# Modulation rows summed by GpSimd in written order beside the attention, totals over partitions later, exponentials in place

## The chip, the cores and the metric

The kernel runs on one core of one Trainium2 chip. The metric is device time of one execution, in microseconds (us). Below, TensorE is also PE, VectorE DVE, ScalarE ACT, GpSimd POOL and SyncE SP, as in the profile.

## The reference

One layer of a diffusion backbone on 1024 latent tokens (x, 1024 wide) with 256 context tokens, all in float32. Cut to what matters here:

```
mod = silu(c) @ w_mod + b_mod                 # w_mod is 1024 x 6144
sh1, sc1, g1, sh2, sc2, g2 = split(mod, 6)    # six rows of 1024
h   = rmsnorm(x, norm1_g) * (1 + sc1) + sh1   # the hidden state
q, k, v, u, B, C, gate_a, gate_c = split(h @ w_in)
o   = windowed attention of q on k, v (16 heads, 4 kv groups, window 128,
      all context keys, a sink logit per head), rope on latent q and k
y   = B * conv3(C * u)
m   = sigmoid(gate_a) * (o @ w_proj_attn) + sigmoid(gate_c) * (y @ w_proj_conv)
x   = x + g1 * (m @ w_out)
h2  = rmsnorm(x, norm2_g) * (1 + sc2) + sh2
x   = x + g2 * expert_choice_moe(h2)          # 16 experts, top 128 tokens each
out = rmsnorm(x, final_norm_g)
```

The rows sh1 and sc1 are needed at the start. The change deals with the other four: g1, sh2, sc2 and g2, parts 2 to 5 of w_mod. Each is a sum over 1024 inputs: 8 blocks of 128 x 1024 weights, each scaled by its column of silu(c), added up, then summed over the 128 partitions, plus the bias.

## The kernel before

Products are made in pairs of float32 parts: a value is split into a rounded high part (ScalarE's copy to the fp32r type) and the rest (a subtraction, mostly VectorE's), and three matmuls make one product. The stages, in the order of the program:

- Norms, the first modulation columns, then the k, v and q projections.
- The attention: 32 units, each one of 4 kv groups and one block of 128 queries with 4 heads. A unit's scores (matmuls L605, L606) get their mask, scale and maximum on VectorE (L608, into a tile `sn`), the exponential on ScalarE (L613, from `sn` into `p`) and, as soon as the softmax sum is there (the small additions L620, L622 and a reciprocal on VectorE), the scaling on GpSimd (L625, four per unit). Then come per 128 keys the transposes (L630), their split (ScalarE L633, VectorE L634) and the values' matmuls (L642, L643). Scores run two units ahead of the values. Between these the function `pour` puts the matmuls of the two gate projections (L40 to L44), whose weights are split into the buffers `whi` and `wlo` (L210), two of each.
- In units 4, 10, 16 and 22 `x_sums` makes on GpSimd the sums and differences of hidden-state blocks that the next stage uses as operands (L657 and L659: ten operations of 512 columns per set), and splits them (L675) into the same `whi` and `wlo`.
- The pair stage: twenty pairs of weight blocks of 128 columns. Two rows of weights and two of data make a 2 x 2 product in seven block products, `product(slot)`, 12 matmuls each (L795). Pairs 0 to 11 are C, u and B of four blocks in turn; pairs 12 to 15 are w_proj_attn, 16 to 19 w_proj_conv. Around the products VectorE and ScalarE make the weights' sums (L829 to L840), their splits (L809, L810), and the outputs (`quad`, L875 to L889; L1107 and L1140 add two products). A B pair also has the convolution of the pair before, four instructions L908 and L910. Before pair 12 and pair 16 the data operands are exchanged one after another (`op_load`, `op_split`, L973 and L974).

In the pair stage the order on all engines is that of the program. `at_turn(n, slot, f)` hangs work behind a product. There hangs the class `Row`: per modulation row eight loads by SP (L740), the scaling on ScalarE (L743), the addition on GpSimd (L745), a split by ScalarE and GpSimd (L751, L752). Its `total` stands ahead of the seventh product of pairs 2, 5, 8 and 12: four matmuls with a column of ones (L760), and VectorE adds the bias row (L761). Also on GpSimd are the differences of attention rows and of y rows that become operands of pairs 12 to 19 (`sums_of`, L930).

Behind it come the output projection with residual and second norm, the router with the choice of tokens, and the experts. The engines' order in the attention is not written out; a scheduler sets it from the program.

## Time and profile before

| | us |
|---|---|
| median of 3 runs (lowest, highest) | 1832.6 (1831.3, 1834.83) |
| the profiled execution, and its span | 1830.33, 1828.5 |
| busy in the span: PE, DVE, ACT, POOL | 1716.5, 1459.1, 1040.5, 557.4 |
| attention, 243 to 575 | 332.0 |
| rest of the gate projections, 575 to 611 | 36.1 |
| pair stage, 611 to 1085 | 474.2 |
| output projection and router, 1085 to 1190 | 104.7 |
| choice of tokens, 1190 to 1230 | 40.0 |
| experts, 1230 to 1828.5 | 598.5 |

Times inside the profile count from the start of the span. The span is shorter than the time of the execution by what lies before its first and after its last instruction, 1.8 us. The granted clock of TensorE is written as a share of 2.4 GHz: 1.00 is 2.4 GHz, 0.50 is 1.2 GHz, and a figure between them is a mean over a stretch that had both. Matmuls overlap, so a start and a duration in a row can reach into the next row.

### The profile page before, as it was taken

What the parts mean: (1) busy time and instruction counts of PE and PEld (TensorE: products, weight loads), DVE (VectorE), ACT (ScalarE), POOL (GpSimd) and SP (SyncE); (2) the same over time, 40 slices, a digit from 0 to 9 for tenths busy, and PEclk for the clock granted to TensorE, in tenths of its full rate; (3) what the DMA queues carried; (4) which work ended last, traced back from release to release, by engine and by line L of the source; (5) the groups of instructions that cost most, each with busy time, mean ns of one, the idle gap of its engine ahead of it and who ended that gap; (6) DMA issues with size and microseconds to landing.
All of it is one profiled execution on the core that took longest, in us unless ns stands there. A gap on an engine that the chain in (4) does not pass through costs nothing.

```text
span 1828.5 us, 24343 instructions
## 1 busy us (share of the span) xinstructions
PE 1716.5 (94%) x8421; PEld 1384.8 (76%) x8421; DVE 1459.1 (80%) x1996; ACT 1040.5 (57%) x1482; POOL 557.4 (30%) x366
## 2 busy tenths in 40 slices
PE   8999999999999989878798898959999999999997
PEld 5778888888888867666567677847888888888875
DVE  6756568778775488897887876578999999999997
ACT  6642267767774334333445343226777877877875
POOL 0001226255231245365763301241024223223101
PEclk8999999999999999998899999979999999999999
DMA  9353354344413737437657245778999999999955
GB/s 343 129 162 115 127 189 142 94 138 126 148 55 121 255 107 220 133 121 230 230 160 252 72 151 190 257 280 323 341 398 396 387 393 399 384 397 398 340 196 196
DMA packets 210861, 415.71 MB, mean 227 GB/s; under 512 B 17643, under 2 KB 107051, under 8 KB 209202
## 3 DMA queue, kind: packets, MB, share of 16 engines
q1 hardware_dynamic: 182226, 368.20, 56.3%
q0 software_dynamic: 6912, 25.51, 4.7%
q10 hardware_dynamic: 21600, 20.45, 3.2%
q8 instruction: 66, 1.08, 0.2%
q14 instruction: 57, 0.47, 0.1%
HBM read 343.31 MB, written 70.80 MB: 226 GB/s over the span
## 4 chain that ended last, share of the span: by engine, by line
PE 63%; DVE 14%; issue 4%; ACT 2%; DMA 2%; POOL 1%; SPq 0%; ACTq 0%; POOLq 0%; DVEq 0%
PE psA L1659 19%; PE psB L1659 5%; PE psF L1659 5%; PE w L795 5%; PE psT L630 3%; PE psT L795 3%; PE psA L1225 3%; PE psF L40 2%; PE psF L42 2%; PE psF L44 2%; PE psB L643 2%; PE psB L642 2%; PE psA L605 2%; PE psA L606 2%; DVE x L810 2%
## 5 line engine op out<-in xcount | busy, mean ns | idle before, releaser
L1659 PE MATMUL psA<-part,xeh 128*128 128x512 f32 x1024 | 281.9, 392 | 0.5 <-ACT xeh L1647 0.5
L1659 PEld LDWEIGHTS psA<-part,xeh 128*128 128x128 f32 x1024 | 191.3, 188 | 39.9 <-ACT xeh L1647 1.0
L1694 POOL DMA_INDIRECT md<-ye,idxs x15 | 107.9, 7190 | 213.3 <-DVE ye L1691 213.3
L1659 PE MATMUL psA<-part,xel 128*128 128x512 f32 x512 | 163.4, 390 | 0.0
L625 POOL TENSOR_SCALAR p<-p,l 128x640 f32<-128x640 f32 (+1 forms) x128 | 99.6, 797 | 176.5 <-DVE l L623 51.3
L1517 DVE TENSOR_TENSOR part<-er,part 128x1024 fp32r<-128x1024 f32 x118 | 138.4, 1219 | 5.3 <-ACT part L1515 2.0
L1515 ACT CAST part<-er 128x1024 fp32r<-128x1024 f32 x118 | 123.7, 1056 | 32.9 <-PE psA L1659 19.9
L809 ACT CAST whi<-raw 128x1024 fp32r<-128x1024 f32 x40 | 42.0, 1049 | 173.7 <-DVE raw L840 110.0
L634 DVE TENSOR_TENSOR tl<-psT,th 128x512 fp32r<-128x512 f32 x152 | 103.9, 687 | 26.5 <-ACT th L633 25.1
L608 DVE CUSTOM_DVE_ANT_0 sn<-psA,msk,nsink 128x640 f32<-128x640 f32 (+1 forms) x128 | 107.3, 843 | 21.7 <-PE psA L606 21.1
L745 POOL TENSOR_TENSOR mp<-mp,mp 128x1024 f32<-128x1024 f32 x28 | 73.3, 2618 | 152.5 <-ACT mp L743 151.7
L633 ACT CAST th<-psT 128x512 fp32r<-128x512 f32 x152 | 88.3, 584 | 50.4 <-PE psT L630 49.5
L613 ACT ACTIVATE p<-sn,nm 128x640 f32<-128x640 f32 (+1 forms) x128 | 103.0, 806 | 19.5 <-DVE nm L608 17.6
L1659 PEld LDWEIGHTS psA<-part,xel 128*128 128x128 f32 x512 | 96.3, 188 | 20.5 <-DVE xel L1648 0.3
L1517 DVE TENSOR_TENSOR part<-mh,part 128x1024 fp32r<-128x1024 f32 x88 | 105.0, 1219 | 5.4 <-ACT part L1515 2.4
L1517 DVE TENSOR_TENSOR part<-ml,part 128x1024 fp32r<-128x1024 f32 x88 | 105.3, 1219 | 4.4 <-ACT part L1515 1.6
L1515 ACT CAST part<-ml 128x1024 fp32r<-128x1024 f32 x88 | 92.2, 1052 | 26.3 <-PE psA L1659 17.6
L1515 ACT CAST part<-mh 128x1024 fp32r<-128x1024 f32 x88 | 92.1, 1052 | 25.2 <-PE psA L1659 16.5
L1517 DVE TENSOR_TENSOR part<-mp,part 128x1024 fp32r<-128x1024 f32 x85 | 100.8, 1220 | 6.6 <-ACT part L1515 3.8
L1515 ACT CAST part<-mp 128x1024 fp32r<-128x1024 f32 x88 | 91.9, 1052 | 24.5 <-PE psA L1659 16.1
L1659 PE MATMUL psB<-part,hhh 128*128 128x512 f32 x256 | 98.6, 396 | 0.2 <-ACT hhh L1647 0.2
L810 DVE TENSOR_TENSOR wlo<-raw,whi 128x1024 fp32r<-128x1024 f32 x40 | 52.9, 1322 | 55.4 <-ACT whi L809 55.4
(501 smaller groups left out, 4695.4 us busy)
## 6 DMA issues: line engine op xcount, KB each, us to landing
raw<-in_w_in_dram SPq DMA_DIRECT2D x49, 512.0 KB, 5.2
er<-in_w_exp_down_dram SPq DMA_DIRECT2D x47, 512.0 KB, 8.7
er<-in_w_exp_up_dram SPq DMA_DIRECT2D x38, 512.0 KB, 6.0
mp<-in_w_exp_gate_dram SPq DMA_DIRECT2D x36, 512.0 KB, 6.3
mh<-in_w_exp_up_dram SPq DMA_DIRECT2D x33, 512.0 KB, 5.6
ml<-in_w_exp_up_dram SPq DMA_DIRECT2D x33, 512.0 KB, 6.5
mp<-in_w_mod_dram SPq DMA_DIRECT2D x32, 512.0 KB, 4.9
er<-in_w_exp_gate_dram SPq DMA_DIRECT2D x32, 512.0 KB, 5.8
```

Of the source, the lines that this page charges most:

```text
L608: nc.vector.tensor_tensor_reduce(out=sn, in0=sp[:, 512 - n:768], in1=msk.rearrange("p a b -> p (a b)")[:, mo * 128:mo * 128 + n + L], op0= ...
L613: nc.scalar.activation(out=p, in_=sn, func=AF.Exp, scale=-1.0, bias=self.nm4[:, h:h + 1], accum_out=self.l4[:, h:h + 1])
L625: nc.gpsimd.tensor_scalar(self.pr[h], self.pr[h], l4[:, h:h + 1], 1.0, op0=OP.mult, op1=OP.mult)
L633: nc.scalar.copy(out=th, in_=pt)
L634: nc.vector.tensor_tensor(out=tl, in0=pt, in1=th.bitcast(F32), op=OP.subtract)
L745: nc.gpsimd.tensor_tensor(out=self.acc, in0=self.w[k], in1=self.acc, op=OP.add)
L795: nc.tensor.matmul(ps_, lhsT=w[a][:, o + k], rhs=xs[b][:, k], start=(first and k + a + b == 0), stop=(k == 3 and a == 1), skip_group_check ...
L810: tt(out=lo, in0=src, in1=hi.bitcast(F32), op=OP.subtract)
L1515: nc.scalar.copy(out=hi, in_=raw)
L1517: eng.tensor_tensor(out=lo, in0=raw, in1=hi.bitcast(F32), op=OP.subtract)
L1659: nc.tensor.matmul(outs[s], lhsT=lh[:, k], rhs=wt[:, s * 512:s * 512 + 512], start=(k == 0 and n == 0), stop=(k == NK - 1 and n == 2))
L1694: nc.gpsimd.indirect_dma_start(out=md, out_offset=bass.IndirectOffsetOnAxis(ap=idxs[:, e:e + 1], axis=0), in_=ye, in_offset=None, compute_ ...
```

## The change

The four rows leave the pair stage. The generator `mod_row` makes a row's weighted sum on GpSimd alone, in pieces: a load by GpSimd's own queue, a scaling and an addition per block, and at the end a store of the 128 x 1024 sum to DRAM (`rowp`). Row 0 runs beside the q projection. Rows 1 to 3 run in the attention as `pool_work`, one or two pieces a unit, followed by the four sets of `x_sums` (now in three pieces each and with scratch tiles of a pool of their own) and by the differences of the first two sets of attention rows. On GpSimd the order within the attention's units is now that of the program.

In the pair stage a row is read back (`row_load`), summed over partitions by two matmuls against a column of `onehot`, so that the two halves of the row land on two partitions (`row_total`), and stored two turns later. The remaining `sums_of` go from GpSimd to VectorE. In the attention the exponential is written over its input (tile `p` takes the place of `sn`) and the sum of the two output halves over `ot`. At the output projection two `quad` calls move behind the router's row.

```diff
+    def mod_row(n, w_tile, acc_tile, more=False):
+        def load(k):
+            row, k = n + 2 + k // NK, k % NK
+            w = w_tile()
+            nc.gpsimd.dma_start(out=w, in_=w_mod[k * 128:(k + 1) * 128, row * 1024:row * 1024 + 1024])
+            rws.append(w)
+        if not rws:
+            load(0)
+            load(1)
+            yield
+        acc = acc_tile()
+        for k in range(NK):
+            w = rws.pop(0)
+            nc.gpsimd.tensor_scalar(w if k else acc, w, sf[:, 0, k:k + 1], 1.0, op0=OP.mult, op1=OP.mult)
+            if k:
+                nc.gpsimd.tensor_tensor(out=acc, in0=w, in1=acc, op=OP.add)
+            if k == NK - 1:
+                nc.gpsimd.dma_start(out=rowp[n], in_=acc)
+            if k < NK - 2 or more:
+                load(k + 2)
+            yield
+    rws = []
...
+    row0 = mod_row(0, lambda: xcp.tile([128, D], F32, name="xt", bufs=2), lambda: xcp.tile([128, 2, D], F32, name="hch")[:, 0])
...
+        if n > 1:
+            next(row0, None)
...
-            sn = at.tile([128, 640], F32, name="sn", bufs=3)[:, 0:n + L]
+            p = at.tile([128, 640], F32, name="p", bufs=12)[:, 0:n + L]
             nc.vector.tensor_tensor_reduce(
-                out=sn, in0=sp[:, 512 - n:768],
+                out=p, in0=sp[:, 512 - n:768],
                 in1=msk.rearrange("p a b -> p (a b)")[:, mo * 128:mo * 128 + n + L], op0=OP.add, op1=OP.min,
                 scale=-0.125, scalar=nsink[:, g * 4 + h:g * 4 + h + 1], accum_out=self.nm4[:, h:h + 1])
-            p = at.tile([128, 640], F32, name="p", bufs=12)[:, 0:n + L]
-            nc.scalar.activation(out=p, in_=sn, func=AF.Exp, scale=-1.0, bias=self.nm4[:, h:h + 1],
+            nc.scalar.activation(out=p, in_=p, func=AF.Exp, scale=-1.0, bias=self.nm4[:, h:h + 1],
...
-                ot = at.tile([64, 512], F32, name="ot", bufs=2)
-                oo = at.tile([64, 512], F32, name="oo", bufs=2)
+                ot = at.tile([64, 512], F32, name="ot", bufs=3)
                 nc.scalar.copy(out=ot, in_=po[64:128])
-                nc.vector.tensor_tensor(out=oo, in0=po[0:64], in1=ot, op=OP.add)
+                nc.vector.tensor_tensor(out=ot, in0=po[0:64], in1=ot, op=OP.add)
...
-        r = [raw_tile(), raw_tile()]
+        r = [w_tile(), w_tile()]
...
         add(t1, t1, t2)
+        yield
...
+    def sums_of(eng, which, ks, p11, p12, p21, p22):
+        for o_, a, b in ((p11, p12, p11), (p12, p22, p12), (p22, p22, p11), (p21, p21, p22)):
+            eng.tensor_tensor(out=o_, in0=a, in1=b, op=OP.subtract)
...
+    def o_rows(ks, p1, p2, eng=nc.sync):
+        eng.dma_start(out=p1, in_=od[ks * 128:(ks + 1) * 128])
+        for th in range(2):
+            eng.dma_start(out=p2[th], in_=od[512 + ks * 128:512 + (ks + 1) * 128, th * 512:th * 512 + 512])
+        return 0, ks, p1[:, 0:512], p1[:, 512:1024], *p2
...
+    def w_tile():
+        return osp.tile([128, 1024], F32, name="w", bufs=2)
...
+    def pool_work():
+        for n in range(1, 4):
+            yield from mod_row(n, w_tile, lambda: osp.tile([128, 1024], F32, name="acc", bufs=2), n < 3)
+        for ks in range(4):
+            yield from x_sums(ks)
+        for ks in range(2):
+            yield from o_sums(ks)
+    def o_sums(ks):
+        o1, o2 = (osp.tile([128, 2, 512], F32, name=nm, bufs=2) for nm in ("acc", "w"))
+        o = o_rows(ks, o1.rearrange("p a b -> p (a b)"), [o2[:, 0], o2[:, 1]], nc.gpsimd)
+        yield
+        sums_of(nc.gpsimd, *o)
+        sums_out(*o)
+        yield
+    pool_left = pool_work()
+    piece = [0]
...
+    pool_order = tc.manual_schedule(engines={mybir.EngineType.Pool})
+    pool_order.__enter__()
...
-        if n in (4, 10, 16, 22):
-            x_sums((n - 4) // 6)
...
             pour(1)
+            if s == 4 or s == 1 and n % 3 == 0:
+                piece[0] += 1
+                assert piece[0] < 37 or n > 24
+                next(pool_left, None)
             if s > 0:
                 cur.values(s - 1)
...
-    class Row:
-
-
-        def __init__(self, n, part):
-            self.n, self.part, self.w = n, part, {}
...
-    def sums_of(which, ks, p11, p12, p21, p22):
-
-        for o_, a, b in ((p11, p12, p11), (p12, p22, p12), (p22, p22, p11), (p21, p21, p22)):
-            nc.gpsimd.tensor_tensor(out=o_, in0=a, in1=b, op=OP.subtract)
...
-        at_turn(3 * m + 4, 2, lambda: sums_of(*st["ys"]))
+        at_turn(3 * m + 4, 2, lambda: sums_of(nc.vector, *st["ys"]))
...
-    for r in range(4):
-        at_turn(3 * r, 0, lambda r=r: row_start(r))
-        for k, (a, b) in enumerate(((0, 2), (1, 3), (2, 4), (5, 7), (6, 8), (9, 11), (10, 12), (13, 15))):
-            at_turn(3 * r, a, lambda k=k: st["row"].load(k))
-            at_turn(3 * r, b, lambda k=k: st["row"].add(k))
-        at_turn(*((3 * r + 2, 2) if r < 3 else (11, 6)), lambda: st["row"].split())
-
-    for ks, b in enumerate((17, 38, 59, 68)):
...
+    def row_load(n):
+        acc, small = mp_slot(4), mp_slot(5)
+        br, nr = small[0:2, 0:512], small[0:2, 512:1024]
+        nc.sync.dma_start(out=acc, in_=rowp[n])
+        nc.sync.dma_start(out=br, in_=b_mod[:, (n + 2) * 1024:(n + 3) * 1024].rearrange("o (h f) -> (o h) f", h=2))
+        if n == 2:
+            nc.sync.dma_start(out=nr, in_=norm2_g.rearrange("o (h f) -> (o h) f", h=2))
+        st["row"] = n, acc, br, nr
+    def row_total():
+        n, acc, br, nr = st["row"]
+        pf = psT()[0:2]
+        for hf in range(2):
+            nc.tensor.matmul(pf, lhsT=onehot[:, 1 - hf:3 - hf], rhs=acc[:, hf * 512:hf * 512 + 512], start=(hf == 0), stop=(hf == 1))
+        tt(out=br, in0=pf, in1=br, op=OP.add)
+        if n == 2:
+            nc.vector.scalar_tensor_tensor(out=br, in0=br, scalar=1.0, in1=nr, op0=OP.add, op1=OP.mult)
+    def row_out():
+        n, acc, br, nr = st["row"]
+        nc.sync.dma_start(out=rowd[n].rearrange("(h f) -> h f", h=2), in_=br)
+    for n in range(4):
+        at_turn(2 * n, 6, lambda n=n: row_load(n))
+        at_turn(2 * n + 2, 2, row_total)
+        at_turn(2 * n + 2, 5, row_out)
+    for ks, b in ((2, 17), (3, 38)):
+        at_turn(0, b - 5, lambda ks=ks: o_late(ks))
+        at_turn(0, b, lambda: sums_of(nc.vector, *st["o"]))
         at_turn(0, b + 3, lambda: sums_out(*st["o"]))
...
-            if n in (2, 5, 8, 12) and slot == 6:
-                st["row"].total([psT(), psT()] if n % 2 == 0 else [psa.tile([128, 512], F32, name=f"w{c}") for c in range(2)])
...
-    for q in (0, 2):
-        prev.quad(q)
...
     bc = router_row()
+    for q in (0, 2):
+        prev.quad(q)
```

Three places in the order of instructions. First VectorE in the third pair (pair 2), from the first convolution instruction to the next pair's sums, before; L761 is the bias row of the total, L839 and L840 are the next pair's sums.

```order
L908 SCALAR_TENSOR_TENSOR mp_6990<-mp_6781,cols,mp_6990 128x1023
L910 SCALAR_TENSOR_TENSOR mp_6990<-mp_6781,cols,mp_6990 128x1023
L908 SCALAR_TENSOR_TENSOR mp_6991<-mp_6782,cols,mp_6991 128x1023
L910 SCALAR_TENSOR_TENSOR mp_6991<-mp_6782,cols,mp_6991 128x1023
L810 TENSOR_TENSOR x_7014<-raw,x_7014 128x512
L1140 TENSOR_TENSOR q<-w_6903,q 128x512
L761 TENSOR_TENSOR mp_6647<-psT,mp_6647 1x512 x2
L839 TENSOR_TENSOR raw<-raw 128x512
```

The bias row stands behind all four convolution instructions here, and the next pair's sums behind the bias row. The same place after, where the same lines are numbered L954 and L956 (convolution), L856 (split), L1185 (sum of two products), L885 and L886 (next sums), L1044 (the total's bias row) and L719 (`sums_of`).

```order
L1044 TENSOR_TENSOR mp_6750<-psT,mp_6750 2x512
L954 SCALAR_TENSOR_TENSOR mp_6970<-mp_6778,cols,mp_6970 128x1023
L956 SCALAR_TENSOR_TENSOR mp_6970<-mp_6778,cols,mp_6970 128x1023
L719 TENSOR_TENSOR mp_6860<-mp_6860 128x512
L719 TENSOR_TENSOR mp_6860<-gs,mp_6860 128x512
L719 TENSOR_TENSOR gs<-gs,mp_6860 128x512
L719 TENSOR_TENSOR gs<-gs 128x512
L954 SCALAR_TENSOR_TENSOR mp_6971<-mp_6779,cols,mp_6971 128x1023
L956 SCALAR_TENSOR_TENSOR mp_6971<-mp_6779,cols,mp_6971 128x1023
L856 TENSOR_TENSOR x_6994<-raw,x_6994 128x512
L1185 TENSOR_TENSOR q<-w_6886,q 128x512
L885 TENSOR_TENSOR raw<-raw 128x512
```

The bias row, for both halves in one instruction, now comes ahead of the convolution and no product of the pair needs it; four differences of attention rows, which GpSimd did before, stand between the two halves of the convolution.

Second, GpSimd in the attention, before: the scalings of three units, the start of the first set of `x_sums` (L657), and the next unit's scalings.

```order
L625 TENSOR_SCALAR p<-p,l_2373 128x640 x4
L625 TENSOR_SCALAR p<-p,l_2511 128x640 x4
L625 TENSOR_SCALAR p<-p,l_2643 128x640 x4
L657 TENSOR_TENSOR raw<-x_696,x_304 128x512
L657 TENSOR_TENSOR raw<-x_697,x_305 128x512
L657 TENSOR_TENSOR raw<-raw 128x512
L657 TENSOR_TENSOR raw<-x_752,raw 128x512
L657 TENSOR_TENSOR raw<-raw,x_753 128x512
L625 TENSOR_SCALAR p<-p,l_2771 128x640 x4
```

With the scalings alone, GpSimd has one group of four per unit. After (L660 is the scaling of the exponentials, L477 and L479 the scaling and addition of a piece of a row, L467 its next load):

```order
L660 TENSOR_SCALAR p<-p,l_2548 128x640 x4
L477 TENSOR_SCALAR w<-w,sf 128x1024
L479 TENSOR_TENSOR acc<-w,acc 128x1024
L467 DMA w<-in_w_mod_dram 128x1024
L477 TENSOR_SCALAR w<-w,sf 128x1024
L479 TENSOR_TENSOR acc<-w,acc 128x1024
L467 DMA w<-in_w_mod_dram 128x1024
L660 TENSOR_SCALAR p<-p,l_2679 128x640 x4
```

Between two units' scalings there are now one or two pieces of a row. Third, GpSimd late in the attention, after, with the semaphores that an instruction waits for; L691 are the subtractions of a set of `x_sums`, whose scratch tiles the set before has to have left.

```order
L660 TENSOR_SCALAR p<-p,l_5312 128x640 [waits DVE_49,PE_49,Activation_49]
L660 TENSOR_SCALAR p<-p,l_5312 128x640 [waits PE_49,Activation_49] x3
L691 TENSOR_TENSOR w<-x_698,x_306 128x512 [waits DVE_49]
L691 TENSOR_TENSOR w<-x_699,x_307 128x512
L691 TENSOR_TENSOR w<-w 128x512 [waits Pool_49]
L691 TENSOR_TENSOR w<-x_754,x_698 128x512 [waits DVE_49]
L691 TENSOR_TENSOR w<-x_755,x_699 128x512
L691 TENSOR_TENSOR w<-w 128x512 [waits Pool_49]
L660 TENSOR_SCALAR p<-p,l_5448 128x640 [waits PE_49] x4
```

The first L691 waits for VectorE, and the four scalings of a unit (L660) stand in the order behind it. Before, the scalings in this place stood one unit behind another.

## Rows read from the trace of the kernel before

**Rows 1.** Busy time by stretch: us, each engine busy (x instructions), PEclk, DMA share, GB/s.
```profile
250.00:575.00 325.00, 322.01 (x1867) 273.35 (x1867) 255.11 (x538) 234.61 (x497) 138.82 (x158) 1.00 0.37 111
611.10:1085.30 474.20, 415.59 (x1698) 326.34 (x1698) 381.22 (x347) 186.95 (x221) 220.88 (x101) 0.94 0.52 168
890.00:930.00 40.00, 24.71 (x84) 16.83 (x83) 36.43 (x22) 18.82 (x21) 26.66 (x9) 0.83 0.44 153
```

**Rows 2.** Chain of waits, pair stage: start, us, what.
```profile
611.32 19.36 PE w L795 x84
630.68 5.50 PE psT L795 x24
...
679.20 7.64 PE psT L795 x24
```

**Rows 3.** Waits of TensorE, 606 to 1095: total us, times, longest.
```profile
PE psT L795 <- DVE mp L761: 13.8, 2, 6.9
PE w L795 <- ACT x L809: 7.5, 2, 4.7
PE w L795 <- DVE mp L761: 6.9, 1, 6.9
...
PE w L795 <- DVE x L810: 4.1, 4, 1.8
PE w L795 <- DVE q L1107: 3.8, 3, 1.7
```

**Rows 4.** Time line of VectorE, 666 to 680: start, us, instruction [idle before].
```profile
667.06 2.57 DVE L908 SCALAR_TENSOR_TENSOR mp<-mp,cols,mp 128x1023 f32<-128x1023 f32 x1 [0.78 <-ACT mp L907]
...
678.48 1.27 DVE L761 TENSOR_TENSOR mp<-psT,mp 1x512 f32<-1x512 f32 x2
```

**Rows 5.** Time line of VectorE, 887 to 901.
```profile
887.21 1.27 DVE L908 SCALAR_TENSOR_TENSOR mp<-mp,cols,mp 128x1023 f32<-128x1023 f32 x1
...
889.72 5.58 DVE L908 SCALAR_TENSOR_TENSOR mp<-mp,cols,mp 128x1023 f32<-128x1023 f32 x1
```

**Rows 6.** Time line of GpSimd, 669 to 672.
```profile
670.86 2.14 POOL L930 TENSOR_TENSOR mp<-gs,mp 128x512 f32<-128x512 f32 x1
```

**Rows 7.** Time line of GpSimd, 889 to 901.
```profile
889.51 10.20 POOL L974 TENSOR_TENSOR t<-t,t 128x2048 fp32r<-128x2048 f32 x2 [3.31 <-ACT t L973]
```

**Rows 8.** Time line of VectorE, 760 to 765.
```profile
760.13 0.68 DVE L889 TENSOR_TENSOR mp<-psF,mp 128x512 f32<-128x512 f32 x1
760.73 0.68 DVE L1107 TENSOR_TENSOR q<-w,q 128x512 f32<-128x512 f32 x1
...
763.78 1.23 DVE L810 TENSOR_TENSOR wlo<-raw,whi 128x1024 fp32r<-128x1024 f32 x1 [1.17 <-ACT whi L809]
```

**Rows 9.** Groups of GpSimd by form: busy us, mean ns, idle before.
```profile
L625 POOL TENSOR_SCALAR p<-p,l 128x640 f32<-128x640 f32 x96 | 77.1, 821 | 127.5 <-PE psT L630 38.7 <-PE psA L606 36.7 <-PE psB L642 31.7
L745 POOL TENSOR_TENSOR mp<-mp,mp 128x1024 f32<-128x1024 f32 x28 | 73.3, 2618 | 152.5 <-ACT mp L743 151.7
```

**Rows 10.** Time line of ScalarE, 843 to 845.
```profile
843.00 1.15 ACT L743 ACTIVATE mp<-mp,sf 128x1024 f32<-128x1024 f32 x1 [5.62 <-DMA mp<-in_w_mod_dram]
```

**Rows 11.** Chain of waits, behind the pair stage.
```profile
1293.10 1.91 PE psT L774 x4
```

**Rows 12.** Time line of TensorE, 668 to 670.
```profile
668.44 1.08 PE L760 MATMUL psT<-mp,onesr 128*1 128x512 f32 x4
```

**Rows 13.** DMA issues of the page: count, size, us to landing.
```profile
mp<-in_w_mod_dram SPq DMA_DIRECT2D x32, 512.0 KB, 4.9
```

**Rows 14.** Time line of VectorE, 432 to 436.
```profile
433.12 1.18 DVE L620 TENSOR_TENSOR es<-sink,nm 128x4 f32<-128x4 f32 x1
```

**Rows 15.** Time line of GpSimd, 432 to 436.
```profile
432.98 1.30 POOL L657 TENSOR_TENSOR raw<-raw 128x512 f32<-128x512 f32 x1
```

**Rows 16.** Time line of TensorE, 437 to 438.5.
```profile
437.43 0.50 PE L643 MATMUL psB<-tl,v2t 128*128 128x512 f32 x1 [1.25 <-DVE tl L634]
```

**Rows 17.** Time line of TensorE, 1105 to 1107.
```profile
1105.97 0.39 PE L1333 MATMUL psT<-identr,bc 16*128 16x16 f32 x2 [1.77 <-DVE bc L1325]
```

More of the change, by code (lines that the diff above doesn't have):

```diff
@@ L192, in small_tables @@
         nc.vector.memset(ones, 1.0)
+        for i in range(3):
+            nc.vector.tensor_scalar(onehot[:, i:i + 1], ones, float(i == 1), None, op0=OP.mult)
     def first_cols():
@@ L563, in hybrid_layer @@
     late()
+    next(row0, None)
+    assert not rws
     pour(16)
@@ L803, in hybrid_layer @@
     NP = len(cols3)
-    onesr = tmpp.tile([128, 2], FR, name="onesr")[:, 0:1]
-    nc.vector.tensor_copy(out=onesr, in_=ones)
     k0, k1 = slice(0, 4), slice(4, 8)
@@ L925, in signal, with o_late @@
             nc.scalar.activation(out=self.sig[q], in_=self.sig[q], func=AF.Sigmoid)
-    def sums_of(which, ks, p11, p12, p21, p22):
-        for o_, a, b in ((p11, p12, p11), (p12, p22, p12), (p22, p22, p11), (p21, p21, p22)):
-            nc.gpsimd.tensor_tensor(out=o_, in0=a, in1=b, op=OP.subtract)
-    def sums_out(which, ks, p11, p12, p21, p22):
-        for n, p in enumerate((p11, p12, p22, p21)):
-            nc.sync.dma_start(out=sums[which][n, ks], in_=p)
-    def o_rows(ks):
-        p1 = mp_slot(7)
-        nc.sync.dma_start(out=p1, in_=od[ks * 128:(ks + 1) * 128])
-        p2 = [stage.tile([128, 512], F32, name="gs", bufs=2) for th in range(2)]
-        for th in range(2):
-            nc.sync.dma_start(out=p2[th], in_=od[512 + ks * 128:512 + (ks + 1) * 128, th * 512:th * 512 + 512])
-        st["o"] = (0, ks, p1[:, h0], p1[:, h1], *p2)
+    def o_late(ks):
+        st["o"] = o_rows(ks, mp_slot(7), [stage.tile([128, 512], F32, name="gs", bufs=2) for th in range(2)])
     takes = (("t1", (tx, "t1")), ("t3", (tx, "t3")), ("b11", (0, 0)), ("b22", (1, 1)), ("t4", (tx, "t4")), ("t2", (tx, "t2")), ("b21", (1, 0)))
@@ L1070, in hybrid_layer @@
     in_order.__enter__()
-    row_start(0)
     cur = Pair(0)
```

44 lines of the change are left out of this document (13 added, 31 removed).

## The prediction, made before the changed kernel was run

> **What bounds the kernel now.** I read the busy table by stretches first. It cuts the run into the attention (250 to 575 us) and the stage of twenty weight pairs (611.1 to 1085.3 us), the two stages that the change rewrites [rows 1]. In the attention TensorE is busy for 322.0 of 325.0 us at a granted clock of 1.00: that stage is bound by TensorE, and GpSimd (138.8 us busy) and VectorE (255.1 us) only have to keep up. In the pair stage TensorE is busy for 415.6 of 474.2 us, the mean granted clock is 0.94 and VectorE is busy for 381.2 us [rows 1]. Twenty pairs of 84 matmuls should take, at the pace of the 84 that the chain of waits shows without a gap (19.36 us) [rows 2], 387 us. So some 85 us of this stage are lost, 59 us as idle TensorE and the rest because the clock falls after each long gap or because of the small matmuls of the row totals.
>
> The list of what TensorE waits for in this stage comes next [rows 3]. The dearest entry is VectorE's addition of the bias row, L761: 13.8 us in two waits and 6.9 us in one. Then come the splits (L809, L810) and the sums L1107. In the chain, 24 matmuls of one kind take 5.50 us, and 7.64 us behind such a wait [rows 2], so each of the three costs another 2.1 us of low clock.
>
> The time line of VectorE shows why L761 is late [rows 4]. It stands behind four convolution instructions, of which the first, at 667.06, takes 2.57 us. The same instruction takes 1.27 us at 887.21, and 5.58 us at 889.72 [rows 5]. What differs is GpSimd: during the four it subtracts attention rows (L930, 2.14 us at 670.86) [rows 6], and during the 5.58 us it runs two 2048-wide subtractions in 10.20 us [rows 7]. Where GpSimd is still, a 512-wide VectorE operation takes 0.68 us and the next begins 0.60 us after it [rows 8]. So in the pair stage GpSimd's work is paid for by VectorE.
>
> **What goes from the pair stage.** (a) The totals with L761 leave slot 6. Three waits, 20.7 us, with 6.4 us of low clock: 27.1 us [rows 2, 3]. (b) The 28 row additions on GpSimd (2.62 us each) [rows 9], four splits and 32 attention and convolution subtractions go, 135 us of GpSimd work; VectorE's pair operations fall back to their undisturbed durations. The waits on L810 and L1107 in ordinary turns are 4.1 and 3.8 us in the list [rows 3]; I take 7.2 us of the 7.9. (c) ScalarE scales the w_mod rows and is in order: at 843.00 it waited 5.62 us for such a row's DMA with a split (L809) behind it [rows 10]; TensorE's longest wait for L809, 4.7 us, follows 10 us later [rows 3]. With 1.4 us of a second wait and 2 us of low clock that is 8.1 us. With no w_mod load left there, this goes. (d) From 890 to 930 us, where the operands change to the attention's output, TensorE is busy for 24.7 of 40 us at a clock of 0.83 [rows 1]. The two convolution instructions there, of which the one shown lost 4.3 us to GpSimd [rows 5, 7], come some 3 us earlier when the additions ahead of them no longer slow VectorE, and may pass before GpSimd's subtractions begin. These subtractions themselves stay. Between nothing and the 15.3 us of idle I take 8. Sum: 50.4 us.
>
> **What comes into it.** (e) Each of four totals is now two matmuls on unsplit fp32. The nearest row is the two fp32 matmuls of the broadcast L774, recorded as four, 1.91 us [rows 11]; the old total's four took 1.08 us [rows 12]. Four times the difference is 3.3 us; it is at best zero. (f) VectorE takes over 24 subtractions of 512, 0.6 us apart, 14.5 us in all. In most pairs they fit: a pair without convolution has 12 to 15 us of VectorE work beside 19.4 us of matmuls. In pairs 2 and 5 they do not: seven product operations and seven sums and splits of 512 (14 by 0.63, 8.8 us), three splits of 1024 (3.5), two waits for a split's other half (2.3) [rows 8], four convolutions (4.9) [rows 5], four subtractions (2.4) and, in pair 2, the bias row (0.7) make 21.9 us in pair 5 and 22.6 us in pair 2, against 19.4 us of matmuls and 21.3 us with a total's 1.91. The next pair's third product then waits for its split: 2.5 and 1.3 us, with low clock about 5 us. Zero if the backlog is eaten by the lighter pair behind; 12 us if all four convolution pairs behave like pair 5.
>
> **What comes into the attention.** GpSimd now runs in written order. Per unit it has four scalings of 0.82 us (3.3 us), and 1.33 pieces of a row: a 1024-wide scaling (about 1.3 us, from the 0.82 us of 640) and an addition of 2.6 us [rows 9], and a load to issue, for which I allow 0.5 us. That is 9.2 us in a unit of about 10.2 us (325 us over 32 units) [rows 1]. Loads are issued two pieces ahead, 8 us or more before use, and land in 4.9 us [rows 13], so they are hidden. Two costs are not. First, VectorE's small additions for the softmax sum (L620, L622) read two SBUF operands. At 433.12 L620 took 1.18 us [rows 14], ending with the GpSimd subtraction that was running (432.98 for 1.30 us) [rows 15], and TensorE waited 1.25 us at 437.43 [rows 16]. In seven units two pieces follow each other and an addition runs just when these come. I take 0.8 us of TensorE for each: 6 us. The Trainium skill (SBUF — State Buffer, "Who interferes with whom") says that a VectorE instruction with two SBUF inputs waits for the whole of a GpSimd instruction that reads SBUF. The trace agrees to 0.02 us here; by it an addition of 2.6 us can hold each of the two for 2.6 us and not 1.3, and seven times both would be 36 us of VectorE, of which TensorE would see the part beyond VectorE's slack; that belongs to the slower case below. Second, the sums of the hidden state now all lie in units 18 to 28. Each set's first subtraction waits for VectorE to have split the set before, which needs one of two buffers that the gate weights also use, and a unit's four scalings stand behind it. By the order of the program the set after next waits about one unit; unit 26's scalings are then ready some 6 us late, and the gate weights' next split about 3.6 us. I take 9 us. The present stalls, some 2.4 us in three of the 3.0 us idle, go. Net 13 us; the bounds are 0 and 40.
>
> **Other places.** The row beside the q projection runs on an idle GpSimd, under matmuls that do not wait: 8 pieces of about 4.5 us end long before the first scores need GpSimd. The exponentials in place take a buffer less and no instruction, nothing. At the output projection two quads move behind the router row, and VectorE's copy at which TensorE waited 1.77 us at 1105.97 [rows 17] comes 4 us earlier: with low clock 3 us gained, at least zero.
>
> **Sum.** -50.4 + 3.3 + 5 + 13 - 3 = -32 us on the profiled execution of 1830.3 us (span 1828.5), 1798 us; the median of the runs lies 2.3 us above it: 1800 us.
>
> **Rivals.** (1) *The backlog, and not the total, held the pairs.* Then the waits at 679, 751 and 822 us come back at the next pair's split or sum. For it: the convolution pairs have as much VectorE work as matmuls. Against it: half of their inflation was GpSimd's. Price: 12 us instead of 5, and the attention at 20 instead of 13: 1814 us. (2) *Slack absorbs the attention's costs.* GpSimd runs a unit ahead and the split waits fall into it (2 instead of 13 us, so no net loss after the present stalls), and (d) is worth 15 us: 1782 us. (3) *GpSimd becomes the attention's bound, slower.* If a piece takes 5 us (additions at 2.9, scalings at 1.6 beside VectorE) and the scalings 1 us each, a unit needs 4 + 1.33 x 5 = 10.7 us plus the time in which GpSimd idles for its unit's sum. From 10.2 us on each unit's transposes wait; at 1.7 us over in 32 units that is 54 us in place of 13: 1841 us. Against it: scalings are 0.82 us in the trace, and the longest wait of GpSimd's in the attention is not for VectorE's slowed part.
>
> **How the numbers follow.** Forecast 0.53, rival 1 0.21, rival 2 0.17, rival 3 0.09. A measurement of this kernel tells about 0.2%, 3.7 us, from no change. Forecast and rival 2 are faster; rival 1 nearly always (0.20 of 0.21); of rival 3 two thirds lie above. Faster 0.89, same 0.03, slower 0.08. The range runs from 1776 us (rival 2 with no cost from (e) and (f)) to 1828 us, which leaves out rival 3 and the far end below. The forecast's own range is 1786 to 1814 us.
>
> **What would show it.** In the profile after: the pair stage about 430 us long, no TensorE wait on a bias row, the convolution instructions near 1.27 us, no wait above 3 us before 890 us; in the attention several TensorE waits of 0.5 to 2 us on VectorE's splits, and one or two of several us between units 24 and 27 on GpSimd's scalings. I am wrong if waits of 5 us and more stand again behind the convolution pairs, or if the attention grows by more than 25 us.

## The result, and the profile after

| | before | after |
|---|---|---|
| median, us (lowest to highest, runs) | 1833.71 (1831.3 to 1837.44, 4) | 1804.44 (1802.18 to 1805.46, 4) |
| the profiled execution, us | 1830.33 | 1805.46 |

The ratio is 0.9837, 95% interval [0.9817, 0.9857]: 29.3 us faster, where 1800 us was forecast. The profiled executions are 24.9 us apart, and the stages share them as follows (cut at TensorE's first or last matmul of each; the output stretch is cut here at the first matmul of the choice of tokens, so it is longer than in the table of stages before).

| stretch | before, us | after, us | difference, us | forecast, us |
|---|---|---|---|---|
| to the last q matmul | 220.6 | 222.6 | +2.0 | 0 |
| from there through attention and gates | 390.3 | 402.1 | +11.8 | +13 |
| pair stage | 474.1 | 429.7 | -44.4 | -42.1 |
| output projection and router | 123.9 | 126.0 | +2.1 | -3 |
| choice of tokens, experts, last norm | 614.2 | 614.8 | +0.6 | 0 |
| from the start of the last VectorE instruction | 5.1 | 8.2 | +3.1 | 0 |

First the stretches of [rows 1] in the profile after (columns as there). The third is the change of operands, which now lies 26 us earlier: it starts, as in [rows 1], within half a microsecond of GpSimd's two 2048-wide subtractions (863.66 us after, 889.51 before).

```profile
250.00:575.00 325.00, 314.52 (x1802) 264.48 (x1802) 259.33 (x525) 228.92 (x485) 249.26 (x238) 0.99 0.49 154
624.90:1054.70 429.80, 410.07 (x1698) 321.43 (x1697) 323.63 (x365) 149.81 (x185) 74.11 (x33) 0.97 0.43 141
864.00:904.00 40.00, 29.56 (x102) 21.08 (x101) 37.09 (x23) 18.78 (x20) 26.98 (x9) 0.87 0.40 141
```

GpSimd's busy time went from the pair stage (220.9 to 74.1 us) into the attention (138.8 to 249.3 us). In the pair stage VectorE is busy for 323.6 us and not 381.2, although it took over 24 subtractions. TensorE idles 19.7 us of it and not 58.6.

The three largest waits of TensorE in the pair stage after, as in [rows 3] (L843 is the product, L1005 and L1006 split the exchanged operands, L855 and L856 the weights):

```profile
PE w L843 <- POOL t L1006: 6.0, 4, 1.9
PE w L843 <- DVE x L1006: 4.0, 1, 4.0
PE w L843 <- ACT x L855: 2.7, 1, 2.7
```

No wait on a bias row is left, and every wait of the stage comes at or behind 868 us, where the first exchange of operands begins. The chain after, against [rows 2]; L1043 is a total:

```profile
625.10 19.46 PE w L843 x84
...
672.30 1.81 PE psT L1043 x4
...
685.37 5.59 PE psT L843 x24
```

The place of the 7.64 us of [rows 2] now takes 5.59 us. VectorE at that place, against [rows 4] (L954, L956 are the convolution, L1185 the pair's last sum):

```profile
681.45 1.28 DVE L954 SCALAR_TENSOR_TENSOR mp<-mp,cols,mp 128x1023 f32<-128x1023 f32 x1
682.77 1.28 DVE L956 SCALAR_TENSOR_TENSOR mp<-mp,cols,mp 128x1023 f32<-128x1023 f32 x1
...
684.57 0.68 DVE L1185 TENSOR_TENSOR q<-w,q 128x512 f32<-128x512 f32 x1
```

The convolution takes 1.28 us where it took 2.57, and VectorE ends the pair at 685.25 us, 0.1 us before TensorE needs the next bank.

In the attention after, VectorE's small addition and GpSimd's addition of a row, against [rows 14] and [rows 15]; then the wait that follows on TensorE ([rows 16]; L655 is L620 of before):

```profile
286.84 1.67 DVE L655 TENSOR_TENSOR es<-sink,nm 128x4 f32<-128x4 f32 x1
```

```profile
286.10 2.39 POOL L479 TENSOR_TENSOR acc<-w,acc 128x1024 f32<-128x1024 f32 x1
```

```profile
289.16 0.50 PE L678 MATMUL psB<-tl,v2t 128*128 128x512 f32 x1 [1.00 <-DVE tl L669]
```

L655 ends at 288.51 us and the addition at 288.49: the 4-element addition lasts as long as GpSimd's. All waits of TensorE from 225 to 625 us, and the largest entry of the same list before (225 to 611 us):

```profile
PE psB L678 <- DVE tl L669: 6.8, 9, 1.2
PE psT L665 <- POOL p L660: 2.2, 2, 1.9
PE psB L677 <- DVE ot L683: 1.1, 1, 1.1
PE psF L40 <- ACT gs L337: 0.9, 2, 0.7
```

```profile
PE psB L643 <- DVE tl L634: 2.4, 3, 1.3
```

### The profile page after: what moved, and what is told of

It reads as the page before. It is cut to its first block, busy times and chain, and to the rows that moved or that the text cites. A ratio compares the mean times of both kernels' runs of the same rounds, so it can differ in the third digit from the quotient of the medians.

```text
span 1803.7 us, 24231 instructions
## 1 busy us (share of the span) xinstructions
PE 1717.8 (95%) x8421; PEld 1381.7 (77%) x8421; DVE 1418.4 (79%) x2018; ACT 1004.7 (56%) x1446; POOL 553.5 (31%) x408
## 3 DMA queue, kind: packets, MB, share of 16 engines
q8 instruction: 66, 1.08, 0.2%
## 4 chain that ended last, share of the span: by engine, by line
PE 81%; DVE 7%; POOL 3%; issue 3%; DMA 3%; ACT 2%; SPq 0%; POOLq 0%; ACTq 0%; DVEq 0%
PE psA L1704 19%; PE w L843 9%; PE psT L843 5%; PE psB L1704 5%; PE psF L1704 5%; PE psA L1268 3%; PE psT L665 3%; PE psF L40 2%; PE psA L401 2%; PE psF L44 2%; PE psF L42 2%; PE psA L399 2%; PE psA L400 2%; PE psF L843 2%; PE psB L678 2%
## 5 line engine op out<-in xcount | busy, mean ns | idle before, releaser
L1739 POOL DMA_INDIRECT md<-ye,idxs x15 | 107.9, 7191 | 213.2 <-DVE ye L1736 213.2
L644 DVE CUSTOM_DVE_ANT_0 p<-psA,msk,nsink 128x640 f32<-128x640 f32 (+1 forms) x128 | 107.8, 843 | 27.4 <-PE psA L642 25.9
L660 POOL TENSOR_SCALAR p<-p,l 128x640 f32<-128x640 f32 (+1 forms) x128 | 101.0, 804 | 57.1 <-DVE l L658 16.0
L648 ACT ACTIVATE p<-p,nm 128x640 f32<-128x640 f32 (+1 forms) x128 | 103.0, 805 | 21.3 <-DVE nm L644 20.6
L927 POOL TENSOR_TENSOR mp<-q,mp 128x512 f32<-128x512 f32 x15 | 24.3, 1648 | 290.8 <-DVE q L921 277.3
L855 ACT CAST whi<-raw 128x1024 fp32r<-128x1024 f32 x40 | 42.0, 1049 | 121.6 <-DVE raw L886 85.3
L1560 ACT CAST part<-mp 128x1024 fp32r<-128x1024 f32 x88 | 92.0, 1053 | 24.9 <-PE psA L1704 16.4
L1704 PE MATMUL psF<-part,hhh 128*128 128x512 f32 x256 | 97.0, 390 | 0.0
```

The costliest lines, as they stand in the source:

```text
L644: nc.vector.tensor_tensor_reduce(out=p, in0=sp[:, 512 - n:768], in1=msk.rearrange("p a b -> p (a b)")[:, mo * 128:mo * 128 + n + L], op0=O ...
L648: nc.scalar.activation(out=p, in_=p, func=AF.Exp, scale=-1.0, bias=self.nm4[:, h:h + 1], accum_out=self.l4[:, h:h + 1])
L660: nc.gpsimd.tensor_scalar(self.pr[h], self.pr[h], l4[:, h:h + 1], 1.0, op0=OP.mult, op1=OP.mult)
L1560: nc.scalar.copy(out=hi, in_=raw)
L1704: nc.tensor.matmul(outs[s], lhsT=lh[:, k], rhs=wt[:, s * 512:s * 512 + 512], start=(k == 0 and n == 0), stop=(k == NK - 1 and n == 2))
L1739: nc.gpsimd.indirect_dma_start(out=md, out_offset=bass.IndirectOffsetOnAxis(ap=idxs[:, e:e + 1], axis=0), in_=ye, in_offset=None, compute_ ...
```

## The experiments

Each kernel was timed in five or more rounds beside the kernel before; the ratios below are to it. The theories are named by the letters of the expectations.

**Undoing the pair stage's other edits.** Totals back at the old place (e1):

```diff
-        at_turn(2 * n + 2, 2, row_total)
...
+            if n in (2, 5, 8, 12) and slot == 6:
+                pfs = [psT(), psT()] if n % 2 == 0 else [psa.tile([128, 512], F32, name="w0")]
+                row_total(pfs[0][0:2])
```

> The changed kernel with the row totals back at their old place, ahead of the seventh product of pairs 2, 5, 8 and 12 and on a bank that the next pair needs first; GpSimd stays quiet in the pair stage. Theory A (GpSimd's work made the bias row late, its place only showed it): VectorE is at most about 1.5 us behind TensorE where a convolution pair ends, so the next pair waits some 2 us each behind pairs 2 and 5 and 0 to 1 us behind 8 and 12, with low clock 4 to 8 us more than the changed kernel's 1804 us. Theory B (the place alone made it): three or four waits near 6.9 us as before, 24 to 30 us more.

The differences back on GpSimd (e2):

```diff
-        at_turn(3 * m + 4, 2, lambda: sums_of(nc.vector, *st["ys"]))
+        at_turn(3 * m + 4, 2, lambda: sums_of(nc.gpsimd, *st["ys"]))
-        at_turn(0, b, lambda: sums_of(nc.vector, *st["o"]))
+        at_turn(0, b, lambda: sums_of(nc.gpsimd, *st["o"]))
```

> The changed kernel with the differences of y rows and of the last two sets of attention rows on GpSimd again instead of VectorE (24 subtractions); totals stay moved. Theory A: the convolution instructions of pairs 2 and 5 rise from 1.28 to about 2.2 us, VectorE is 1 to 2 us later there, and TensorE sees little of it, 0 to 5 us more than 1804 us. Theory C (what held the pairs was VectorE's backlog by contention, with or without a total): waits of 5 us and more on splits behind pairs 2 and 5, 10 to 16 us more.

Both edits (e3):

> Both of the former: totals at the old place and the 24 subtractions on GpSimd. Against the kernel before only the additions and loads of the rows are missing from the pair stage. Theory A: the two act together, two waits of 5 to 7 us behind pairs 2 and 5 (behind pair 8 none, its attention rows went into the attention), 14 to 20 us more than 1804 us, more than the sum of the two alone. Theory B: the same as the total at its old place alone, 24 to 30 us. Rival (the 28 additions of rows and their scalings held VectorE and ScalarE): under 8 us.

Measured: e1 1805.61 us, ratio 0.9842 [0.9824, 0.9859]; e2 1803.79, 0.9833 [0.9816, 0.9851]; e3 1802.78, 0.9836 [0.9817, 0.9856]. None can be told from the changed kernel. Theory B falls with e1: with the rows' sums gone from GpSimd, the totals cost nothing at their old place; nor did theory A's 4 to 8 us come there. The prices that theories A and C put on the differences (14 to 20 us in e3, 10 to 16 us in e2) did not come either, but the collision that they priced did not take place. In e3 the differences ran from 652 us, ahead of the convolution, since nothing stood before them in GpSimd's queue, and in e2 from 653 us; in both the convolution took 1.28 us. These runs show that the 24 differences cost nothing at that time, and leave open what they cost beside the convolution.

```profile
652.44 1.29 POOL L719 TENSOR_TENSOR mp<-mp 128x512 f32<-128x512 f32 x1 [59.70 <-DVE raw L876]
```

Of theory A its core is left, that GpSimd's work makes the bias row late, and of e3's expectation the rival (under 8 us, the additions).

**Taking the rows' sums out of the kernel before.** Scalings and additions (f1, which returns ahead of the scaling too), then the additions alone (f3, the diff shown):

```diff
             nc.scalar.activation(out=self.w[k], in_=self.w[k], func=AF.Copy, scale=sf[:, 0, k:k + 1])
-            if k:
-                nc.gpsimd.tensor_tensor(out=self.acc, in0=self.w[k], in1=self.acc, op=OP.add)
-            else:
+            if not k:
```

> The kernel before with ScalarE's scalings and GpSimd's additions of the modulation rows left out (the rows' sums are not made; loads, splits, totals at the old place and all 32 differences on GpSimd stay). Theory D (the additions stood ahead of the differences in GpSimd's queue, pushed them beside the convolution, and with ScalarE's waits for the loads made up nearly all of the loss): no wait on a bias row above 1 us, the pair stage 428 to 436 us as in the three former experiments, 38 to 46 us less than before. Theory B (place of the total) or A (differences on GpSimd): the waits near 6.9 us stay, at most 15 us less than before.

> The kernel before with only GpSimd's 28 additions of rows left out (ScalarE still scales every block; the rows' sums are not made). Theory D: nearly as the former run without sums, 30 to 44 us less than before; what is left of the difference to it is ScalarE's waits for the blocks' loads, up to 8 us. Rival (ScalarE's scalings and waits in its order are the main cost): less than 15 us gained, waits on splits behind ScalarE all over the stage.

Measured: f1 1802.15 us, 0.982 [0.9805, 0.9835]; f3 1804.81, 0.9832 [0.9817, 0.9848]. To leave out GpSimd's 28 additions, and nothing else, brings as much as the whole change. That the two are equal is chance: f3 pays nothing in the attention, where the change loses 11.8 us, and keeps a longer pair stage. f1 gains 32.3 us in the median, less than the 38 to 46 us that theory D expected, and f3 29.6 us. Three waits on the bias row stay, at 4.2 us each in f3 (6.9 before):

```profile
PE psT L793 <- DVE mp L759: 8.4, 2, 4.2
...
PE w L793 <- DVE mp L759: 4.2, 1, 4.2
```

(L793 and L759 are L795 and L761 of before.) The row's split is still on GpSimd there, and the differences behind it, and the convolution of pairs 2, 5 and 8 is as slow as before: in pair 2 its four instructions take 2.57, 2.20, 2.31 and 2.19 us, against 2.57, 2.20, 2.29 and 2.17. That is 4.1 us more than four times 1.28, about what TensorE still waits. So theory D has the wrong mechanism. The additions did not cost by pushing the differences beside the convolution (none of them ran beside these twelve instructions before), but by holding VectorE elsewhere in the stretch.

```profile
662.39 2.44 POOL L750 TENSOR_TENSOR mp<-mp,mp 128x1024 fp32r<-128x1024 f32 x1 [93.47 <-ACT mp L749]
663.34 2.57 DVE L906 SCALAR_TENSOR_TENSOR mp<-mp,cols,mp 128x1023 f32<-128x1023 f32 x1 [0.78 <-ACT mp L905]
```

**Moving the wait, or the work, in the kernel before.** The totals on the banks that are needed last (f2):

```diff
-... .total([psT(), psT()] if n % 2 == 0 else [psa.tile([128, 512], F32, name=f"w{c}") for c in range(2)])
+... .total([psB(), psF()] if n % 2 == 0 else [psa.tile([128, 512], F32, name=f"w{c}") for c in (2, 3)])
```

> The kernel before with one edit: the row totals write the two banks that the next pair needs last instead of the two that it needs first, so that no product waits for the bias row at once. Theory B (the wait on the bias row was the loss): three waits of 6.9 us go, 20 to 27 us less than before. Theory D: VectorE stays 4 to 5 us late behind the convolutions, and the next pair's third product waits for its split or its bank instead, 0 to 8 us less than before.

Measured: 1835.62 us, 1.0007 [0.9996, 1.0018]. The bias row is gone from the list of waits, theory B's 20 to 27 us are not gained, and this has taken its place (the second entry was 7.5 us before, [rows 3]; the first was not there):

```profile
PE psF L795 <- ACT x L809: 12.3, 2, 6.8
PE w L795 <- ACT x L809: 11.2, 4, 4.0
```

The differences ahead of the split in GpSimd's queue (f4):

```diff
-    for ks, b in enumerate((17, 38, 59, 68)):
+    for ks, b in enumerate((15, 36, 57, 66)):
```

> The kernel before with one edit of four numbers: the differences of attention rows are called two products earlier, so that in GpSimd's queue they stand ahead of the row's split and no longer behind it; all work, the totals' place and the additions stay. Theory D (what GpSimd's queue runs beside the convolution sets the loss there): the differences end before about 666 us, only the split (2.5 us) lies beside the convolution, the four convolution instructions take 1.3 to 2 us, and the three waits on the bias row fall from 6.9 to 2 to 4 us: 10 to 16 us less than before. Rival (the split and the total make the loss by themselves, wherever the differences stand): 6.9 us stays, within 4 us of before.

Measured: 1832.71 us, 0.9995 [0.9982, 1.0008], against 10 to 16 us less expected. The waits on the bias row did fall, to at most 1.7 us, and three of the four convolution instructions of pair 2 took 1.28 us. But the loss moved: most of it into the product sums of the pair's start (5.1 us in all before), beside which the differences now run, and some into waits on splits (L809, L810). The two largest entries on the sums:

```profile
PE w L795 <- DVE q L1107: 7.9, 2, 4.1
...
PE psT L795 <- DVE q L1107: 4.0, 1, 4.0
```

The rows there also show which VectorE instructions pay. L875 reads PSUM (`psT`) and took 0.68 us beside a subtraction of GpSimd. L889, with two SBUF operands, took 1.07 us behind it, and 0.69 us at the same place before, where GpSimd was still:

```profile
659.92 1.74 POOL L930 TENSOR_TENSOR mp<-mp 128x512 f32<-128x512 f32 x1
660.44 0.68 DVE L875 TENSOR_TENSOR q<-psT,q 128x512 f32<-128x512 f32 x1
661.15 1.07 DVE L889 TENSOR_TENSOR mp<-q,mp 128x512 f32<-128x512 f32 x1
```

What decides is thus how much of GpSimd's work runs beside VectorE over the whole stretch, and the instruction at which TensorE is seen to wait is only where VectorE's lateness comes out. The first eleven pairs (from the L1107 sum of pair 0 to that of pair 11, read by stretch):

| | length, us | DVE busy | POOL busy | clock |
|---|---|---|---|---|
| before | 264.1 | 212.1 | 134.5 | 0.95 |
| f2, other banks | 265.2 | 213.2 | 134.5 | 0.94 |
| f4, differences earlier | 261.7 | 203.8 | 129.5 | 0.95 |
| f3, no additions | 238.0 | 165.2 | 57.5 | 0.97 |
| f1, no scalings either | 234.5 | 167.7 | 60.5 | 0.98 |
| after | 222.2 | 156.5 | 1.8 | 1.00 |
| e3, differences on GpSimd | 220.2 | 145.4 | 31.2 | 1.00 |

The rows of before, f3 and e3:

```profile
616.90:880.96 264.06, 230.56 (x951) 181.98 (x950) 212.10 (x187) 96.91 (x111) 134.52 (x63) 0.95 0.52 167
```

```profile
617.86:855.81 237.95, 223.25 (x939) 178.46 (x938) 165.24 (x187) 97.55 (x111) 57.46 (x36) 0.97 0.57 185
```

```profile
631.00:851.19 220.19, 220.19 (x939) 174.40 (x938) 145.44 (x184) 61.09 (x76) 31.24 (x22) 1.00 0.36 115
```

From before to f3 GpSimd is busy for 77.1 us less (70.4 us of additions, and its other instructions are shorter too). This takes 46.9 us off VectorE, with the same 187 instructions on it, and 26.1 us off the stretch; ScalarE's scalings are 3.5 us more. The last 14.3 us, from f1 to e3, go with the split, the old total and the differences that stood behind the split; no run tells these three apart. The three waits on the bias row that f1 keeps, 4.3 us each, are 12.9 us of it. In e3 TensorE never idles in this stretch, and 31 us of GpSimd's work cost nothing.

**The attention.** Rows 1 to 3 not summed there (e4):

```diff
-            nc.gpsimd.tensor_scalar(w if k else acc, w, sf[:, 0, k:k + 1], 1.0, op0=OP.mult, op1=OP.mult)
-            if k:
+            if n == 0 or k == 0:
+                nc.gpsimd.tensor_scalar(w if k else acc, w, sf[:, 0, k:k + 1], 1.0, op0=OP.mult, op1=OP.mult)
+            if k and n == 0:
```

> The changed kernel without the scalings and additions of modulation rows 1 to 3 in the attention beyond each row's first block (their loads stay; these rows' sums are left out). Theory A (GpSimd's additions hold VectorE's two small additions of the softmax sum): the six waits of 0.5 to 1.0 us before 400 us, 5.1 us in all, go; the waits between 525 and 565 us stay; 5 to 7 us less than 1804 us. Rival (a unit's scalings queue behind pieces of a row in GpSimd's written order, all over the attention): 10 to 13 us less.

Measured: 1800.7 us, 0.9811 [0.9792, 0.9831]. From the last q matmul to the last gate matmul it takes 395.2 us, against 402.1 us after and 390.3 us before: the rows' arithmetic costs 6.9 us of the attention's 11.8, by theory A. (The median is only 3.7 us below the changed kernel's, where 5 to 7 us were expected; the profile has the longer of the two lengths of the expert stage that the last section tells of.) The waits on VectorE's split before 480 us are gone, while the one of 1.93 us on GpSimd's scalings (at 523 us) stays and one of 0.84 us (at 536 us) is new. The other 4.9 us lie where the sums of the hidden state run in written order; that these sums cost them is argued from the place of the waits, and no run took them out.

Pieces spread (g_att):

```diff
-        for n in range(1, 4):
+        for n in range(2, 4):
...
-            if s == 4 or s == 1 and n % 3 == 0:
+            if s == 4:
```

> The changed kernel with GpSimd's pieces spread: two rows beside the q projection, two in the attention, one piece a unit, and each set of hidden-state sums split at its own end, a unit before the next set starts. If two pieces in one unit and the wait for the former split are what the attention lost: VectorE's two small additions take at most 0.3 us, the waits of 0.5 to 1.9 us of TensorE in the attention fall to a total under 4 us (from 10.4), the gate matmuls end 6 to 9 us earlier; 1796 to 1799 us. If a piece anywhere costs the same: within 2 us of 1804 us, the loss only moves into the q projection.

Measured: 1808.6 us, 0.9865 [0.9848, 0.9882]. That is slower than the changed kernel, if by little: the two intervals overlap, but all five times (from 1805.9 us) lie above its four (to 1805.5 us). VectorE's two small additions are back at 14.5 us in all, from 29.4, and the attention is 4.7 us shorter (397.3 us). The 6 to 9 us expected are not reached: TensorE now waits for an output of the gates (2.4 us) and ScalarE's copies instead (9.1 us of waits in all, from 11.0), and the second row lengthens the q projection by 2.4 us. So 2.3 us were gained up to the pair stage in the profile, 2.7 us up to the experts, and an expert stage of the longer kind (566.7 us for 563.6) took them back. Why the other four times are higher still stays open.

**The output projection.** The quads back (h), then x loaded first (g_out):

```diff
     bc = router_row()
-    for q in (0, 2):
-        prev.quad(q)
```

> The changed kernel with the two output quads at the output projection back at their old place, ahead of the router's row. If the move cost what the trace after shows (the load of x waits for a tile that these quads read; TensorE's wait of 4.9 us on the residual in place of 1.8, 0.5 and 0.5 us): the wait on the router's row of 1.8 us is back, the long one is under 1 us, and the stretch from the first output matmul to the choice of tokens is 2 us shorter, 124 instead of 126 us. If the move gained the 3 us of the forecast and something else cost 5 us, it is 3 us longer, 129 us.

```diff
+    for t in range(2):
+        xs[t] = raw_tile()
+        nc.sync.dma_start(out=xs[t], in_=x[t * 128:(t + 1) * 128])
     g1r = stage.tile([128, 1024], F32, name="wlo", bufs=2)
     bcast_row(g1r, rowd[0:1])
```

> The changed kernel with one edit at the output projection: the loads of the first two blocks of x are issued ahead of the broadcast loads of the modulation rows instead of behind them. If SyncE's order holds the residual (the load of x waits in the queue behind a row's load, whose tile the moved quads still read): the wait of 4.9 us on the residual falls to 1 to 2 us, 2 to 4 us less than the changed kernel's 1804 us. If x waits for a tile of its own that comes free late: no change.

Measured: h 1803.88 us, 0.9829 [0.9814, 0.9845], and the stretch takes 126.3 us, as after (126.0): neither expectation held. The wait on the residual fell from 4.92 to 2.69 us and that on the router's row stayed small (0.25 us), but the quads' place is worth nothing either way. g_out 1802.79 us, 0.9832 [0.9815, 0.9848]; its stretch takes 122.3 us, 3.7 us less, and the wait fell into the 1 to 2 us expected. After, SyncE's queue and the wait on TensorE:

```profile
1074.83 0.33 SPq L826 DMA_DIRECT2D wlo<-rowd  x1
1075.49 0.80 SPq L826 DMA_DIRECT2D whi<-rowd  x2
1076.39 2.27 SPq L1273 DMA_DIRECT2D raw<-in_x_dram  x3
...
1084.68 1.54 PE L1312 MATMUL psT<-identr,raw 128*128 128x128 f32 x6 [4.92 <-DVE raw L1278]
```

And in g_out:

```profile
1067.87 1.47 SPq L1239 DMA_DIRECT2D raw<-in_x_dram  x2
1072.70 0.33 SPq L826 DMA_DIRECT2D wlo<-rowd  x1
...
1079.35 0.87 PE L1316 MATMUL psT<-identr,raw 128*128 128x128 f32 x6 [1.72 <-DVE raw L1282]
```

x stood in SyncE's queue behind a row's load whose tile the quads still read: that load waited 12.7 us for a quad's sum (L921), and 11.8 us already in the kernel before. Freed from it the wait is 1.72 us. The median is 1.7 us below the changed kernel's, and that can't be told from no change.

**Everything together** (g_all: g_att, g_out and e3):

> All that helped, in one kernel: pieces spread as in the run before, x loaded ahead of the rows, the totals at their old place and the 24 differences on GpSimd. If the parts add up: 6 to 9 us from the attention, 2 to 4 from the output projection and 2 from the pair stage, 1789 to 1794 us.

Measured: 1805.57 us, 0.9839 [0.9821, 0.9856]. The parts did not add up: the first eleven pairs take the 220.2 us of e3, but the first pair starts 3.4 us later than after, because the spread pieces lengthen the q projection here by 5 us. Up to the experts the profile is 3.4 us ahead of the changed kernel's, where 10 to 15 us were expected, and its expert stage is of the longer kind too (566.9 us). No version tried can be told from the changed kernel on the better side; e3 and g_out have the lowest medians of those that leave nothing out.

## Why the prediction was right, point by point

The direction and the main cause were right: GpSimd's work in the pair stage was paid by VectorE, and moving it costs the attention less than it saves. That the number came so near is in part luck. Terms of the pair stage that were too large and too small cancelled, and the median's 29.3 us stands beside 24.9 us between the two profiled executions, for which the sum had 32. Of these 7 us the output projection has 5, the row beside the q projection 2 and the end of the span 3; the pair stage gave 2 us more than forecast and the attention 1 us.

**The pair stage, (a) to (f).** Forecast -42.1 us, measured -44.4. Up to pair 11 the terms (a), (b), (c), (e), (f) came to -34.1 us, and 41.9 us went. The sum held, but not its reasons. Term (a) put 27.1 us on the bias row and its place. f2 took that place away and gained nothing, e1 gave it back and lost nothing: it was VectorE's lateness by GpSimd's work, and the total was where it came out, as the first rival said of the pairs. That rival's price was wrong, since the lateness itself went. Term (b) was much too small: it had 7.2 us, and 26.1 us hang on the additions alone (f3), 8.1 us of them as the part of the three waits on the bias row that goes. The prediction looked for the lateness in the four convolution instructions, beside which no addition runs; by f3 these are worth some 4 us of each wait of 6.9. The first of them, its line at 667.06, ran beside the row's split (L752, 2.50 us from 666.05) and not beside the subtractions. Term (c) was not tested by itself; the scalings as a whole are worth 3.5 us (f3 to f1), where 8.1 us stood. In (f) nothing of the 5 us came, although its sum of VectorE's work was right: pair 2 took VectorE 23.3 us, from 661.92 to 685.17, beside 21.4 us of matmuls from 663.99. What the term left out is VectorE's lead. It began 2.1 us before the pair's first matmul, and the third product of the next pair, from 690.96 us, came 0.8 us after its split (VectorE's time line, then the chain):

```profile
661.92 0.68 DVE L885 TENSOR_TENSOR raw<-raw 128x512 f32<-128x512 f32 x1
688.91 1.22 DVE L856 TENSOR_TENSOR x<-raw,x 128x1024 fp32r<-128x1024 f32 x1
```

```profile
663.99 8.31 PE w L843 x36
690.96 2.72 PE psF L843 x12
```

To move the 24 subtractions onto VectorE was not needed (e2). The Trainium skill (Perfetto Trace Analysis, "Optimizing Scalar/DVE Operations") says that moving operations between GpSimd and VectorE may not help, since the two share a read port; e2 agrees, 0.9833 against 0.9837.

**(d), the exchange of operands.** Forecast -8 us, measured -2.6 us from pair 11 on; TensorE's idle time in the 40 us of the exchange fell by 4.9 us, from 15.3 to 10.4. The convolution did pass before GpSimd's two 2048-wide subtractions, which took 9.68 us after ([rows 7]: 10.20). But a split of 512 and a sum behind it took 5.08 and 4.45 us instead, so the loss moved to the next instructions with two SBUF operands.

```profile
863.66 9.68 POOL L1006 TENSOR_TENSOR t<-t,t 128x2048 fp32r<-128x2048 f32 x2 [7.72 <-PE psB L843]
863.84 5.08 DVE L856 TENSOR_TENSOR x<-raw,x 128x512 fp32r<-128x512 f32 x1
869.44 4.45 DVE L885 TENSOR_TENSOR raw<-raw 128x512 f32<-128x512 f32 x1
```

**(e), the totals.** 1.81 us each against 1.08: 2.9 us, forecast 3.3.

**The attention.** Forecast +13 us, measured +11.8. Waits on VectorE's small additions: 6 us forecast; the waits for the split behind them come to 6.8 us, 5.2 of them before 400 us, and e4 gives 6.9 us. One small addition took up to 2.39 us, as long as an addition of GpSimd. Behind the sums of the hidden state: 9 us less the present stalls of 2.4, against the 4.9 us that e4 leaves. Of the waits named for units 24 to 27, one of 1.94 us on GpSimd's scalings came, at 531 us, where one or two of several us were forecast. Of the third rival there is no sign: a piece took 4.15 us (1.17 + 2.40 + 0.58), not 5.

**Costed at nothing.** The row beside the q projection cost 2.0 us. The cover named was an idle GpSimd and matmuls that do not wait; VectorE's split of k, which matmuls do wait for, was overlooked. After, its two instructions take 2.95 us, beside an addition of 2.40 us from 130.67 us on; the same two take 1.29 us at 102 us, with GpSimd still:

```profile
131.27 2.95 DVE L433 TENSOR_TENSOR kl<-t,kh 128x512 fp32r<-128x512 f32 x2 [1.09 <-ACT kh L432]
...
133.76 0.50 PE L438 MATMUL psT<-identr,kl 128*128 128x128 f32 x4 [0.96 <-DVE kl L433]
```

The output projection should have gained 3 us and lost 2.1: the wait on the router's row of [rows 17] went, and TensorE waited for x instead. The step that failed took the wait away without asking what is late next.

One bound of the prediction was added up wrongly: rival 2 without (e) and (f) is 1774 us and not 1776. Nothing hung on it.

## To carry to other kernels

When TensorE waits for the last VectorE instruction of a stretch, sum up what slowed VectorE over the whole stretch before pricing that instruction: moving it, or giving it another bank, moved the wait and not the time. Work on two SBUF operands on GpSimd was paid here by VectorE instructions with two SBUF operands (46.9 us for 77.1, 0.61 us for each of GpSimd's). It cost the kernel nothing where VectorE had slack (e3), so that is where to put it. For an experiment, leave out the suspected work first: f3 alone showed where most of the loss came from, when moving work and waits about had gained nothing.

## What the runs showed of the hardware

The expert stage, which no run changes, has two lengths: 563.2 to 563.6 us in eight profiles, 566.7 to 567.1 us in six. The change's own profile and e1's show them, with the same number of matmuls and a lower clock in the longer one:

```profile
1212.60:1776.21 563.61, 562.73 (x2682) 462.55 (x2682) 538.07 (x563) 444.36 (x465) 122.77 (x30) 1.00 0.94 353
```

```profile
1209.62:1776.34 566.72, 565.96 (x2682) 465.02 (x2682) 538.10 (x563) 444.63 (x465) 121.46 (x30) 0.99 0.93 351
```

There is one profile of each kernel, so no run tells whether the kernel or the execution sets the length; but the times of a single kernel spread as far (e3: 1801.8 to 1807.8 us). These 3.5 us hide differences of the size of g_out's. And the span runs on for 8.2 us from the start of the last VectorE instruction in every kernel made from the changed one, for 5.1 us in every one made from the kernel before, with the same eight stores of the output. No run tells why.
